# A Strassen matmul on one core: a pair of groups in another order, and small sums moved from GpSimd to VectorE

## The chip, the cores and the metric

The kernel runs on one core of a Trainium2 chip. The metric is the time of one execution on the device, in microseconds. Five engines work side by side, each with a queue of its own that it works through in order: TensorE (PE) multiplies, VectorE (DVE) and ScalarE (ACT) compute elementwise, GpSimd (POOL) does so more slowly, and SyncE (SP) issues the transfers. They wait for each other by semaphores that are set when the program is built.

## The reference

```
cs = np.cumsum(x, axis=1)                     # x: 8 x 2048 x 2048 float32
diff = cs - (cs shifted by one row, a zero row first)
return np.matmul(diff, w)                     # w: 2048 x 2048 float32
```

The difference of the running sum is x again, so the output is x times w, 16384 x 2048 by 2048 x 2048.

## The kernel before

**The arithmetic.** The rows of x are cut into 128 tiles of 128 rows. Four tiles are computed as plain products at the start while w is loaded, the next eight in two transitional groups; from then on 29 equal **groups** of four tiles follow (`Group`, L988). In a group the tiles are called g, h, k, l. Each tile's 2048 columns are cut in two halves, and w in four blocks, so that tiles g and k, or h and l, make a 2 x 2 block matrix. The group computes it by Strassen's scheme in Winograd's form: seven block products, P1 to P7, in place of eight. P1, P2, P3, P4 and P5 are cut once more in the same way, into seven quarters p1 to p7 each (a step of four matmuls of 128 x 512); P6 is computed whole, in eight steps of four matmuls; P7 is whole in even groups and by seven in odd ones (`onto`, L1082). Products accumulate in the eight PSUM banks (b0 to b7).

**A step's name.** `1:P1.p7` is quarter p7 of P1 in the odd group of a pair, `0:` the even group. What else stands around the matmuls:

- `load`, `weigh0/1`, `scale`, `recip`, `unit`, `narrow0/1`, `turn0/1`: a tile of x is loaded in two halves, ACT sums the absolute values of its rows (L125), DVE makes a scale of it (L141, L150) and POOL the factor for the way back (L155), ACT rounds the tile to f16 in place (L166), and a transposing transfer turns it (L179). SP issues loads, turns and the stores `put` (L612) from one queue.
- `S1` to `S4` are sums of whole tile halves, and `P1.s1` to `P5.s4`, `P7.s1` to `s4` the **small sums** of x of 128 x 512 in f16 that the inner seven need (`small_sums`, L1033). Each runs on DVE (L561) or, if its name stands in `ON_POOL`, on POOL (L559).
- `fp4` and the like: DVE makes a weight of 128 x 2048 for a quarter just in time, in the one buffer `flow` (L957).
- `cg`, `ct`, `cv` (L1056) and P7's `c1` to `c7` (L1088): ACT copies a partial product out of a bank, to another bank or to an SBUF buffer c. `m1`, `m2`, `a1` to `a7k` (L1063): DVE **merges** such a copy into a bank. A product's seven quarters go on in the same bank once copy or merge have read it.
- `keep` (ACT, L598 or L1118) starts an output piece in a buffer c from a bank, `add` (DVE, L601 or L1129) adds another bank to it, `last` (ACT, L598) scales it, `put` stores it. There are eight buffers c, taken and given back in the order in which the steps are written.

Where ACT and DVE read one bank after each other, the second waits for the first to end, as for a true dependence.

**What sets the order.** `Group` only makes a table of named steps. A list of names, `ORDER` (L1272), holds each step of a pair of groups once, with `+1` or `+2` for the pair whose step it is; the loop at L1367 goes through the list once per pair and runs each step's code, and so fills the queues of all five engines. `after` (L86) keeps each engine's instructions in the order of writing. 415 names make a pair. The last group's P4 has a list of its own, `END_ORDER`.

Of the kernel before, what the change touches and what calls it, by code (L numbers as in the profile page):

```python
# [10 lines left out]
def kernel(  # L11
# [1279 lines left out]
    1:scale.l+1 1:recip.l+1 1:narrow0.l+1 1:turn0.l+1 1:S1.g+1 1:keep.C11g1+1 1:P2.s4+1
    1:narrow1.l+1 0:last.C21g1+1 1:P2.p2+1 1:add.C11g0.v+1 1:put.C11g0+1 1:P2.p6+1
    1:P1.p4+1 1:turn1.l+1 0:add.C21h1.q+1 0:put.C21g1+1 1:P2.p5+1 1:S2.g+1
    1:add.C11g1.q+1 1:P6g.2+1 0:keep.C21h0+1 1:keep.C11h0+1 1:unit.l+1 1:P2.s3+1
    1:P2.p7+1 1:keep.C11h1+1 1:S4.g+1 1:P2.fp4+1 1:add.C11h1.q+1 1:P6g.3+1
    0:add.C21h0.x+1 1:add.C11h1.e+1 1:P5.p1+1 1:P6g.1+1 0:load.g+2 1:S1.h+1 1:P5.s1+1
    1:P5.cg+1 1:P2.p4+1 1:S2.h+1 0:last.C21h1+1 1:P2.p3+1 1:P5.p2+1 1:keep.C22g0+1
# [112 lines left out]
```

## Time and profile before

| | |
|---|---|
| three runs, median (lowest, highest) | 1508.2 us (1507.02, 1510.32) |
| profiled execution | 1507.86 us, of which the span 1505.6 us |
| PE busy | 1446.9 us, 96% |
| DVE, ACT, POOL busy | 1321.8, 1115.9, 460.9 us |
| granted clock of PE | 1.00 |
| transfers on SP's queue | 84.5% of 16 engines' span |

In the rows below, a group of instructions reads: line, engine, operation, output and inputs by the program's names, shapes, count, then busy time and mean duration in ns, then the idle time of the engine just before them and what ended it. A row of the table of waits has who waited, for whom, the total in us, how often, and the longest. A row of the timeline has start, duration, engine, line and operation, with the idle time ahead of it in brackets.

### The profile page before, as it was taken

To read this page: it belongs to the slowest core of one execution; us is meant where nothing else is said; L and a number is where in the kernel's file an instruction comes from. 1 tells how busy PE (TensorE), PEld (TensorE's weight loads), DVE (VectorE), ACT (ScalarE), POOL (GpSimd) and SP (SyncE) were. 2 spreads that over 40 slices of the span, in tenths; PEclk is the share of its full clock that TensorE was granted. 3 is DMA by queue.
4 is the path that set the end of the run, shared out by engine and by line. 5 is a ranking of instruction groups with operands and counts; after the bars stand their busy time and mean duration, and the time that the engine had idled before them with its cause. 6 is when DMAs were issued, how large, how long until landed. Compare 5 with 4: busy or idle time off the path is not lost. (4 is left out here: it accounts for less than half of the span.)

```text
span 1505.6 us, 20953 instructions
## 1 busy us (share of the span) xinstructions
PE 1446.9 (96%) x6617; PEld 644.1 (43%) x6623; DVE 1321.8 (88%) x2166; ACT 1115.9 (74%) x1726; POOL 460.9 (31%) x440
## 2 busy tenths in 40 slices
...
DMA packets 377760, 351.65 MB, mean 234 GB/s; under 512 B 274800, under 2 KB 274800, under 8 KB 377520
## 3 DMA queue, kind: packets, MB, share of 16 engines
q1 hardware_dynamic: 377088, 348.47, 84.5%
...
## 5 line engine op out<-in xcount | busy, mean ns | idle before, releaser
L590 PE MATMUL b<-W,x 128*128 128x512 f16 x2004 | 485.8, 379 | 14.6 <-DVE c L1129 8.9
L590 PEld LDWEIGHTS <-x 128*128 128x128 f16 x2712 | 263.5, 98 | 349.2 <-issue 26.7
L571 PE MATMUL b<-W,x 128*128 128x512 f16 x1696 | 393.5, 379 | 0.1
L1129 DVE TENSOR_TENSOR c<-b,c 128x512 f32<-128x512 f32 x504 | 337.5, 683 | 60.4 <-ACT c L1118 37.6
L166 ACT ACTIVATE F<-F,of 128x1024 f16<-128x1024 f32 x246 | 283.2, 1151 | 42.9 <-DVE of L150 40.2
L125 ACT ACTIVATE waste<-F 128x1024 uint8<-128x1024 f32 x246 | 259.5, 1055 | 37.1 <-DMA F<-in_x_dram 35.6
L590 PEld LDWEIGHTS <-inner 128*128 128x128 f16 x1816 | 176.8, 98 | 254.0 <-issue 25.6
L590 PE MATMUL b<-W,inner 128*128 128x512 f16 x1000 | 251.6, 379 | 26.9 <-DVE b L1063 22.3
L598 ACT ACTIVATE c<-b,of 128x512 f32<-128x512 f32 x268 | 178.3, 684 | 133.4 <-PE b L590 59.4
L571 PEld LDWEIGHTS <-x 128*128 128x128 f16 x1696 | 165.7, 98 | 200.9 <-DVE x L561 1.9
L601 DVE SCALAR_TENSOR_TENSOR c<-b,of,c 128x512 f32<-128x512 f32 x286 | 208.4, 744 | 24.9 <-ACT c L598 11.0
L561 DVE TENSOR_TENSOR x<-x,x 128x1024 f16<-128x1024 f16 (+1 forms) x345 | 208.4, 612 | 20.4 <-PE b L571 14.7
L559 POOL TENSOR_TENSOR inner<-x,inner 128x512 f16<-128x512 f16 x87 | 115.4, 1327 | 335.9 <-DVE inner L561 230.9
L590 PE MATMUL b<-flow,x 128*128 128x512 f16 x700 | 179.7, 379 | 3.8 <-DVE flow L957 3.3
L598 ACT ACTIVATE c<-c,of 128x512 f32<-128x512 f32 x224 | 158.6, 721 | 18.9 <-DVE c L1129 18.9
L1118 ACT COPY c<-b 128x512 f32<-128x512 f32 x224 | 127.6, 583 | 39.7 <-PE b L571 20.3
L559 POOL TENSOR_TENSOR inner<-x 128x512 f16<-128x512 f16 x58 | 76.6, 1320 | 261.0 <-DVE x L561 145.3
L1063 DVE TENSOR_TENSOR b<-b,c 128x512 f32<-128x512 f32 x200 | 137.1, 693 | 17.0 <-ACT c L1056 14.3
L155 POOL TENSOR_SCALAR of<-of,uw 128x1 f32<-128x1 f32 x124 | 74.5, 611 | 185.8 <-DVE of L141 178.3
L590 PE MATMUL b<-inner 128*128 128x512 f16 x472 | 118.7, 379 | 1.2 <-ACT c L598 0.8
L957 DVE TENSOR_TENSOR flow<-W 128x2048 f16<-128x2048 f16 x86 | 113.1, 1315 | 0.0
L559 POOL TENSOR_TENSOR inner<-inner,x 128x512 f16<-128x512 f16 x58 | 77.8, 1341 | 75.8 <-PE b L590 58.8
...
## 6 DMA issues: line engine op xcount, KB each, us to landing
...
out_dram<-c SPq DMA_DIRECT2D x492, 256.0 KB, 3.5
...
W<-in_x_dram SPq DMA_DIRECT2D x16, 256.0 KB, 7.1
...
out_dram<-o POOLq DMA_DIRECT2D x5, 256.0 KB, 4.0
out_dram<-o SPq DMA_DIRECT2D x5, 256.0 KB, 3.4
...
```

Of the source, the lines that this page charges most:

```text
L125: lambda: nc.scalar.activation(waste, where[t][i], ABS, scale=1.0 / ROW, accum_out=sums_of[t][:, i : i + 1],),
L166: lambda: nc.scalar.activation(narrowed(t)[:, ds(i * NH, NH)], where[t][i], COPY, scale=s),
L559: after("pool", lambda: nc.gpsimd.tensor_tensor(dst.all, p.all, q.all, op))
L561: after("dve", lambda: nc.vector.tensor_tensor(dst.all, p.all, q.all, op))
L571: said = nc.tensor.matmul(to[n], a[k], b[k][:, n, :], start=(first and k == 0), stop=(k == KH - 1), skip_group_check=True,)
L590: said = nc.tensor.matmul(to, a[k], b[k], start=(first and k == 0), stop=(k == 3), skip_group_check=True)
L598: after("act", lambda: nc.scalar.activation(c, p, COPY, scale=u))
L601: after("dve", lambda: nc.vector.scalar_tensor_tensor(c, p, u, c, MUL, ADD))
L957: after("dve", lambda: nc.vector.tensor_tensor(flow_all, x, y, op))
L1063: after("dve", lambda: nc.vector.tensor_tensor(t, p, s, ADD))
L1118: after("act", lambda: nc.scalar.copy(to, p))
L1129: after("dve", lambda: nc.vector.tensor_tensor(to, p, to, ADD))
```

## The change

Two tables are replaced, and no code. `ORDER` holds the same 415 names in another order (with `+0`, `+1` and `+2`, since the list begins at another point of the pair). `ON_POOL` holds 8 names in place of 21: six of the old ones and two new ones (1:P3.s3, 1:P7.s4), while fifteen become instructions of DVE. The lines after `ON_POOL` have numbers lower by two, those after `ORDER` by one: L561 is L559, L1063 is L1061, L1129 is L1127.

```diff
     ON_POOL = """
-    0:P1.s1 0:P1.s3 0:P1.s4 0:P2.s1 0:P2.s2 0:P2.s3 0:P2.s4 0:P3.s2 0:P4.s3 0:P5.s4
-    1:P2.s1 1:P2.s2 1:P2.s3 1:P2.s4 1:P3.s1 1:P3.s2 1:P3.s4 1:P4.s2 1:P4.s3 1:P4.s4
-    1:P5.s4
+    0:P1.s1 0:P2.s1 1:P3.s1 1:P3.s3 1:P3.s4 1:P4.s2 1:P4.s4 1:P7.s4
     """.split()
...
     ORDER = """
...
-    0:keep.C21h1+1 0:add.C12g1.e+1 0:keep.C21g0+1 0:add.C12h1.e+1 1:P1.s2+1 1:P1.p5+1
-    1:P1.cg+1 0:last.C12g1+1 1:unit.k+1 1:P1.s4+1 0:put.C22g0+1 0:P4.p6+1 0:put.C12h0+1
-    0:P4.s3+1 1:P1.ct+1 0:keep.C21g1+1 0:add.C21h1.e+1 1:P1.fp4+1 0:put.C22h1+1
-    1:P1.p6+1 1:load.l+1 1:turn0.k+1 1:narrow1.k+1 1:P1.s3+1 1:turn1.k+1 1:P1.m1+1
-    1:weigh0.l+1 0:add.C21g0.x+1 0:P4.p3+1 1:P1.p2+1 0:add.C21g1.x+1 1:P1.p7+1 1:P2.p1+1
...
-    0:recip.g+2 1:P7.fp6+1 1:P7.c5+1 1:keep.C12h1+1 1:P5.s4+1 1:P5.p6+1 1:P7.p2+1
-    1:P5.m1+1 1:add.C22g0.x+1 1:P7.s4+1 1:P7.p6+1 1:P5.p7+1 0:narrow0.g+2 0:narrow1.g+2
-    1:P7.a5g+1 1:P7.c6+1 1:P5.m2+1 1:P5.p3+1 1:put.C22g0+1 1:keep.C22h1+1 1:P4.p2+1
-    1:P3.s2+1 1:P3.s4+1 0:weigh1.h+2 1:add.C12h1.z+1 1:P7.a6+1 1:keep.C12h0+1
-    1:keep.C22g1+1 1:P3.p1+1 0:turn0.g+2 1:P7.fp4+1 1:add.C12g0.q+1 0:scale.h+2
-    0:turn1.g+2 1:last.C12g0+1 1:put.C12g0+1 1:P7.p3+1 1:add.C22g1.x+1 1:P7.p4+1
-    1:P7.fp7+1 1:P3.p3+1 1:add.C12g1.z+1 1:P3.p6+1 1:P7.p7+1 1:P4.p1+1 0:recip.h+2
...
+    0:add.C12g1.e+1 1:P1.s3+1 0:put.C22g0+1 0:P4.p1+1 0:P4.p3+1 0:put.C12h0+1
+    0:keep.C21g1+1 1:unit.h+1 0:keep.C21h1+1 0:add.C12h1.e+1 0:add.C21h1.e+1
+    0:last.C12g1+1 1:P2.s1+1 1:P1.s2+1 1:P1.cg+1 1:P1.p5+1 1:P1.s4+1 0:keep.C21g0+1
+    1:narrow1.k+1 1:P1.ct+1 1:P1.p6+1 0:add.C21g1.x+1 1:load.l+1 0:P4.p6+1 1:P1.p2+1
+    1:P1.m1+1 0:add.C21g0.x+1 0:last.C12h1+1 1:P2.s2+1 0:add.C21g1.q+1 1:turn1.k+1
+    1:P1.fp4+1 1:turn0.k+1 1:P2.p1+1 1:P1.p7+1 1:P1.m2+1 1:P2.s3+1 1:P2.cv+1
...
+    1:P7.p5+1 0:weigh1.h+2 1:P7.c1+1 1:P7.a1+1 1:last.C11g1+1 1:P5.p5+1 1:P7.fp6+1
+    1:P5.s4+1 1:keep.C12g1+1 0:scale.h+2 1:put.C11h1+1 1:P5.ct+1 1:P7.c5+1 1:P5.p6+1
+    1:unit.l+1 1:P5.m1+1 0:recip.g+2 1:P7.p2+1 1:add.C22g0.x+1 1:P3.s1+1 1:P7.a5g+1
+    0:put.C21h0+1 1:P7.s4+1 1:P7.p6+1 1:put.C11g1+1 1:P5.p7+1 1:P4.p2+1 1:P7.c6+1
+    1:P5.p3+1 1:keep.C12h1+1 0:recip.h+2 1:P7.a6+1 1:P3.s3+1 1:P5.m2+1 1:put.C22g0+1
+    0:narrow0.g+2 0:unit.g+2 1:keep.C12h0+1 1:keep.C22h1+1 1:P7.fp4+1 1:keep.C22g1+1
+    1:P3.s2+1 1:P7.p3+1 0:turn0.g+2 1:add.C12h1.z+1 1:add.C22g1.x+1 1:P7.p4+1
+    1:put.C22g1+1 1:P3.p1+1 1:P3.s4+1 1:P7.fp7+1 0:narrow1.g+2 1:add.C12g0.q+1
+    0:narrow0.h+2 1:P3.p3+1 1:add.C12g1.z+1 0:narrow1.h+2 1:last.C12g0+1 1:P7.p7+1
...
```

**DVE around the odd group's merge P1.m1.** The first row is add.C12h1.e of the even group; b2 is the bank of add.C21h1.e, `flow<-W,S` is P1.fp4, the L1063 row is P1.m1. Before:

```order
L1129 TENSOR_TENSOR c2_755<-b7_791,c2_755 128x512
L561 TENSOR_TENSOR inner_779<-inner_779,x00_63 128x512
L561 TENSOR_TENSOR inner_779<-x00_63,inner_779 128x512
L1129 TENSOR_TENSOR c5_767<-b2_786,c5_767 128x512
L957 TENSOR_TENSOR flow_783<-W_58,S1_775 128x2048
L561 TENSOR_TENSOR inner_779<-x00_63,x10_65 128x512
L1063 TENSOR_TENSOR b2_786<-b5_789,c3_759 128x512
```

And of the change, with P1.s3 (`x00_63,x10_65`) as the first row and P1.fp4 as the last:

```order
L559 TENSOR_TENSOR inner_779<-x00_63,x10_65 128x512
L1127 TENSOR_TENSOR c1_751<-b3_787,c1_751 128x512
L1127 TENSOR_TENSOR c0_747<-b2_786,c0_747 128x512
L559 TENSOR_TENSOR inner_779<-x11_66 128x512
L559 TENSOR_TENSOR inner_779<-inner_779,x00_63 128x512
L559 TENSOR_TENSOR inner_779<-x00_63,inner_779 128x512
L1127 TENSOR_TENSOR c3_759<-b7_791,c3_759 128x512
L1061 TENSOR_TENSOR b2_786<-b4_788,c5_767 128x512
L599 SCALAR_TENSOR_TENSOR c2_755<-b0_784,of_8085,c2_755 128x512
L559 TENSOR_TENSOR inner_779<-inner_779,x01_64 128x512
L1127 TENSOR_TENSOR c3_759<-b6_790,c3_759 128x512
L955 TENSOR_TENSOR flow_783<-W_58,S1_775 128x2048
```

P1.fp4 and P1.s3 stood between add.C21h1.e and the merge; now P1.s3 is ahead of the add and P1.fp4 behind the merge.

**ACT at the same place.** The copy that reads the bank b2 is keep.C21g1; the first L1056 row is P1.cg, the second P1.ct. Before:

```order
L1118 COPY c5_767<-b1_785 128x512
L598 ACTIVATE c4_763<-b6_790,of_8073 128x512
L1056 COPY b7_791<-b5_789 128x512
L598 ACTIVATE c1_751<-c1_751,of_7858 128x512
L1056 COPY c3_759<-b1_785 128x512
L1118 COPY c0_747<-b2_786 128x512
```

And of the change, where the L1054 rows are the same two copies (keep.C21g1 is the first row):

```order
L1116 COPY c3_759<-b2_786 128x512
L1116 COPY c0_747<-b5_789 128x512
L596 ACTIVATE c4_763<-c4_763,of_7854 128x512
L1054 COPY b5_789<-b4_788 128x512
L596 ACTIVATE c2_755<-b6_790,of_8085 128x512
L166 ACTIVATE F_62<-F_62,of_8386 128x1024
L1054 COPY c5_767<-b3_787 128x512
```

keep.C21g1 was the last of the six and is now the first of the seven; narrow1.k (L166) now stands ahead of P1.ct.

**DVE from the odd group's merges P7.a5g to P7.fp7.** Before (the rows are P7.a5g, P5.m2, add.C12h1.z, P7.a6, P7.fp4, add.C12g0.q, scale.h, add.C22g1.x, P7.fp7):

```order
L1063 TENSOR_TENSOR b2_786<-b2_786,c5_767 128x512
L1063 TENSOR_TENSOR b0_784<-b6_790,c3_759 128x512
L1129 TENSOR_TENSOR c1_751<-b0_784,c1_751 128x512
L1063 TENSOR_TENSOR b2_786<-b2_786,c4_763 128x512
L957 TENSOR_TENSOR flow_783<-W_58,flow_783 128x2048
L1129 TENSOR_TENSOR c0_747<-b0_784,c0_747 128x512
L141 TENSOR_SCALAR of_8623<-of_8623 128x1
L601 SCALAR_TENSOR_TENSOR c4_763<-b2_786,of_8390,c4_763 128x512
L957 TENSOR_TENSOR flow_783<-W_58 128x2048
```

And of the change (P7.a5g, recip.h, P7.a6, P5.m2, P7.fp4, P3.s2, add.C12h1.z, add.C22g1.x, P7.fp7):

```order
L1061 TENSOR_TENSOR b2_786<-b2_786,c6_771 128x512
L150 RECIPROCAL of_8617<-of_8617 128x1
L1061 TENSOR_TENSOR b2_786<-b2_786,c2_755 128x512
L1061 TENSOR_TENSOR b1_785<-b0_784,c4_763 128x512
L955 TENSOR_TENSOR flow_783<-W_58,flow_783 128x2048
L559 TENSOR_TENSOR inner_779<-inner_779,x01_64 128x512
L1127 TENSOR_TENSOR c1_751<-b1_785,c1_751 128x512
L599 SCALAR_TENSOR_TENSOR c0_747<-b2_786,of_8386,c0_747 128x512
L955 TENSOR_TENSOR flow_783<-W_58 128x2048
```

add.C12h1.z moves from ahead of P7.a6 and P7.fp4 to behind them, and the small sum P3.s2, which POOL did, stands between.

**POOL from the odd group's P3.s1 on.** Of the change (P3.s1, P7.s4, P3.s3, unit.g, P3.s4, P4.s2, P4.s4, then P1.s1 and P2.s1 of the next even group):

```order
L557 TENSOR_TENSOR inner_779<-x11_66 128x512
L557 TENSOR_TENSOR inner_779<-x00_63,inner_779 128x512
L557 TENSOR_TENSOR x11_66<-x01_64,x11_66 128x512
L155 TENSOR_SCALAR of_8588<-of_8588,uw_59 128x1
L557 TENSOR_TENSOR inner_779<-x01_64,inner_779 128x512
L557 TENSOR_TENSOR x20_67<-x20_67,x21_68 128x512
L557 TENSOR_TENSOR x30_69<-x21_68,x20_67 128x512
L557 TENSOR_TENSOR inner_779<-x10_65 128x512
L557 TENSOR_TENSOR inner_779<-x11_66 128x512
```

These eight are all the sums that POOL does in a pair, where it did 21; the others are now L559 rows of DVE, as in the places above.

More of the change, by code (lines that the diff above doesn't have):

```diff
@@ L1291 @@
[L1291 to L1297, printed above, removed]
@@ new lines @@
+    1:turn0.g+1 0:P5.s3+1 0:add.C12g0.z+1 0:P3.s2+1 0:P3.s4+1 1:weigh1.h+1 1:turn1.g+1
+    0:P5.m1+1 0:last.C12g0+1 0:last.C11g1+1 1:weigh0.h+1 0:P5.fp4+1 1:scale.h+1
+    1:recip.h+1 0:P6h.3+1 0:P3.p6+1 0:add.C12g1.q+1 0:put.C11g1+1 0:P6h.2+1 0:P5.p7+1
+    0:P5.p3+1 0:P3.p7+1 0:keep.C12h0+1 0:add.C22g0.x+1 0:P5.m2+1 0:put.C12g0+1
+    0:keep.C12h1+1 0:P4.s1+1 0:S3.h+1 0:keep.C22h1+1 0:put.C11h0+1 0:add.C12h1.z+1
+    0:add.C12h1.q+1 0:keep.C22g1+1 0:P5.p4+1 1:narrow0.h+1 0:P4.fp4+1 0:P7h.2+1
```

89 lines of the change are left out of this document (44 added, 45 removed).

## The prediction

> **What bounds the kernel now.** First the page, for who is busy; then the groups of instructions with shapes kept apart, for where TensorE (PE) stands idle; then the table of waits; then the chain of waits, for the length of one pair of groups; last the timeline of the two places where PE stands longest.
>
> ```profile
> span 1505.6 us, 20953 instructions
> ...
> PE 1446.9 (96%) x6617; PEld 644.1 (43%) x6623; DVE 1321.8 (88%) x2166; ACT 1115.9 (74%) x1726; POOL 460.9 (31%) x440
> ```
>
> The profiled execution took 1507.86 us, 2.3 us more than its span; I make the sum against it. The median of the three runs is 1508.2 us, 0.3 us higher. PE sets the end, but VectorE (DVE) is at 88%.
>
> ```profile
> 1192.80 3.45 PE b L571 x16
> ...
> 1228.87 7.07 PE b L590 x32
> ...
> 1320.36 7.07 PE b L590 x32
> ...
> 1412.72 7.07 PE b L590 x32
> ```
>
> The first row gives PE's pace: 3.45 us for 16 matmuls, 0.216 us each, so 0.863 us for a step of four. A pair of groups has 51 + 50 steps (each of P1 to P5 has seven per group, P6 eight, P7 eight in the even and seven in the odd group), 101 x 0.863 = 87.1 us. The other three rows are the same stretch of three successive pairs: (1412.72 - 1228.87) / 2 = 91.9 us. So nearly 5 us of each pair is PE standing still.
>
> ```profile
> L590 PE MATMUL b<-W,x 128*128 128x512 f16 x2004 | 485.8, 379 | 14.6 <-DVE c L1129 8.9 <-DVE b L1063 4.5 <-ACT c L598 0.8
> ...
> L590 PE MATMUL b<-W,inner 128*128 128x512 f16 x1000 | 251.6, 379 | 26.9 <-DVE b L1063 22.3 <-ACT c L1118 3.3 <-DVE c L1129 0.2
> ...
> L590 PE MATMUL b<-flow,x 128*128 128x512 f16 x700 | 179.7, 379 | 3.8 <-DVE flow L957 3.3
> ```
>
> ```profile
> DVE c L1129 <- ACT c L1118: 37.6, 29, 2.3
> ...
> PE b L590 <- DVE b L1063: 26.8, 20, 1.9
> ...
> PE b L590 <- DVE c L1129: 9.2, 16, 0.7
> ...
> PE b L590 <- ACT c L1118: 3.3, 13, 0.3
> PE b L590 <- DVE flow L957: 3.3, 14, 0.2
> ```
>
> The three groups have 45.3 us of idle PE. A matmul's row is 0.379 us long where the pace is 0.216, so each wait hides another 0.163 us; 20 + 16 + 13 + 14 waits hide 10.3 us. Together about 55 us: the most that any order can win. Four fifths of it is DVE being late: the merges (L1063) and the adds (L1129).
>
> One pair, at the odd group's P1.p7 (DVE, ACT, GpSimd and PE in turn):
>
> ```profile
> 1040.01 0.42 DVE L561 TENSOR_TENSOR inner<-x,inner 128x512 f16<-128x512 f16 x1
> 1042.47 0.69 DVE L1129 TENSOR_TENSOR c<-b,c 128x512 f32<-128x512 f32 x1 [2.04 <-ACT c L1118]
> 1043.08 1.22 DVE L957 TENSOR_TENSOR flow<-W,S 128x2048 f16<-128x2048 f16 x1
> 1044.21 1.38 DVE L561 TENSOR_TENSOR inner<-x,x 128x512 f16<-128x512 f16 x1
> 1045.51 0.69 DVE L1063 TENSOR_TENSOR b<-b,c 128x512 f32<-128x512 f32 x1
> ...
> 1041.84 0.60 ACT L1118 COPY c<-b 128x512 f32<-128x512 f32 x1
> ...
> 1043.12 2.19 POOL L559 TENSOR_TENSOR inner<-inner,x 128x512 f16<-128x512 f16 x1 [3.43 <-PE b L590]
> ...
> 1041.96 1.03 PE L590 MATMUL b<-S,inner 128*128 128x512 f16 x4
> 1042.83 1.89 PE L590 MATMUL b<-W,x 128*128 128x512 f16 x8
> 1046.25 1.02 PE L590 MATMUL b<-W,inner 128*128 128x512 f16 x4 [1.54 <-DVE b L1063]
> ```
>
> Read it backwards. P1.p7 waits 1.54 us (1.70 with the hidden part) for merge P1.m1. The merge is late because three instructions stand ahead of it on DVE: P1.fp4, the small sum P1.s3, and add.C21h1.e, for which DVE stood idle 2.04 us until ACT's copy keep.C21g1 had read the same bank. P1.s3 took 1.38 us, about a microsecond too long, while a sum of GpSimd (POOL), itself 2.19 us long, stood beside it.
>
> **The change part by part.**
>
> (a) The wait at P1.p7. Between P1.p6 and P1.p7 PE now has P4.p6, P1.p2 and P2.p1, 3 x 0.863 = 2.59 us instead of 1.73. On ACT keep.C21g1 is ahead of P1.cg and P1.ct rather than behind them, and on DVE three small sums and an add stand between add.C21h1.e and the merge, while P1.fp4 and P1.s3 are out of the way. After P1.p6 the merge has at most one add, 0.68, and itself, 0.69, to go: 1.4 us, well under 2.59. I take the whole 1.70 us as gone, in 14 odd groups: -23.8 us. Bounds: half of it stays (-11.9), if the merge is then late for P1.ct instead; the other end is the value itself.
>
> (b) The waits at P3.p1 and P7.p4 of the odd group.
>
> ```profile
> 1073.00 0.69 DVE L1129 TENSOR_TENSOR c<-b,c 128x512 f32<-128x512 f32 x1 [0.81 <-ACT c L598]
> ...
> 1073.75 1.02 PE L590 MATMUL b<-W,x 128*128 128x512 f16 x4 [0.57 <-DVE c L1129]
> ...
> 1075.86 1.04 PE L590 MATMUL b<-flow,x 128*128 128x512 f16 x4 [0.23 <-DVE flow L957]
> ```
>
> Here merge P5.m2, ACT's keep.C22h1 and DVE's add.C12h1.z use one bank in turn, 0.69 us each, behind P5.p7, and P3.p1 needs that bank: 2.1 us and the hops against two steps, 1.73. Now four steps stand between P5.p7 and P3.p1 (3.45 us), and P7.fp4 and P3.s2 run on DVE while ACT reads: 0.69 + 1.22 + 0.42 + 0.69 = 3.0. The wait of 0.57 + 0.16 goes: 14 x 0.73 = -10.2 us. P7.p4 has four steps since P7.p6 where it had five, but its weights (P7.fp4) no longer stand behind add.C12h1.z: copy 0.6, P7.a6 0.69, P5.m2 0.69, P7.fp4 1.22 make 3.2 us against 3.45. Its 0.23 + 0.16 goes too: 14 x 0.39 = -5.5 us. Bounds for both together: 0 and -15.7; they go where the DVE queue has no new delay, so I take the full value and put the delay into (c).
>
> (c) A new loop through a result buffer. P7.fp7 now stands behind add.C22g1.x, this behind keep.C22g1 on ACT, and that one needs the buffer that put.C22g0 frees: in the old order keep.C22g1 took a buffer that DVE had freed.
>
> ```profile
> out_dram<-c SPq DMA_DIRECT2D x492, 256.0 KB, 3.5
> ```
>
> From P5.p5 to P7.p7: two ACT copies 1.1, P5.m1 0.69, add.C22g0.x 0.74, the landing 3.5, keep 0.69, add 0.74, P7.fp7 1.22, the hops some 0.4: 9.1 us. PE has ten steps between, 8.63 us. So 0.5 us of new stall, and the DVE work queued behind (P5.fp4, the P7 merges, the adds that free the next group's banks) is late with it; I take 0.8 us a pair, 14 x 0.8 = +11.2 us. Bounds: 0, if the landing is a microsecond shorter than the median; and 0.8 + 2.1 us a pair, +41 us, if it takes the 5.6 us that the page gives for a load of twice the bytes.
>
> (d) POOL does 8 small sums of a pair where it did 21 (two of the eight are new to it), so DVE does 13 more.
>
> ```profile
> L559 POOL TENSOR_TENSOR inner<-x,inner 128x512 f16<-128x512 f16 x87 | 115.4, 1327 | 335.9 <-DVE inner L561 230.9 <-PE b L590 103.7
> ...
> L957 DVE TENSOR_TENSOR flow<-W 128x2048 f16<-128x2048 f16 x86 | 113.1, 1315 | 0.0
> ...
> L957 DVE TENSOR_TENSOR flow<-W,inner 128x2048 f16<-128x2048 f16 x58 | 70.8, 1220 | 15.5 <-PE b L590 15.5
> ...
> L559 POOL TENSOR_TENSOR inner<-x,x 128x512 f16<-128x512 f16 x44 | 50.9, 1157 | 0.0
> ...
> L561 DVE TENSOR_TENSOR inner<-x 128x512 f16<-128x512 f16 x73 | 41.9, 574 | 3.4 <-DMA x<-F 2.4
> ...
> L561 DVE TENSOR_TENSOR inner<-x,x 128x512 f16<-128x512 f16 x16 | 16.3, 1017 | 0.0
> L561 DVE TENSOR_TENSOR x<-x 128x512 f16<-128x512 f16 x30 | 12.5, 418 | 0.0
> ```
>
> POOL's sums (five groups, 304 in all; the first and the last are shown) become 8 x 14 plus two for the last even group, 114: 190 fewer. An undisturbed sum is 418 ns on DVE: 190 x 0.418 = +79 us. Against that, DVE's f16 instructions run long where POOL works: 86 x (1315 - 1220) + 73 x (574 - 418) + 16 x (1017 - 418) ns = 29 us; in proportion 190/304 of it, 18 us, goes. Net +61 us of DVE time, 4.3 us a pair. One stretch of a pair's length shows what room there is (PE, its weight loads, DVE, ACT, POOL):
>
> ```profile
> 1032.00:1123.50 91.50, 88.72 (x407) 39.61 (x406) 80.86 (x135) 70.00 (x111) 30.89 (x29) 1.00 0.83 226
> ```
>
> DVE is idle 10.6 us of it, so the 4.3 lie in waits that it has anyway: on the path I count 0. If that cover is gone it costs up to 61 us.
>
> The Trainium skill, "SBUF — State Buffer", section "Who interferes with whom", says that a VectorE instruction with two SBUF inputs and a GpSimd instruction that reads SBUF exclude each other, the first to issue holding the shared port to its end. The 1.38 and the 2.19 us above agree with it. It also speaks against this change: it makes a rival below.
>
> (e) The head, before the pairs, and the last P4 keep their code: 0. SP's puts and turns keep their number; what a put's new place costs is in (c).
>
> Sum: 1507.9 - 23.8 - 10.2 - 5.5 + 11.2 = 1479.6. I say **1480 us**.
>
> **Rivals.**
>
> *The locks gather.* Of the eight sums left, P3.s4, P4.s2, P4.s4 of the odd and P1.s1, P2.s1 of the next even group stand close together, in the stretch of loop (c), beside P7.fp7, P5.fp4 and DVE's own sums. If one full POOL sum, 1.16 us at worst and about 1.0 as P1.s3 showed, falls on the path in each pair: +14 us, 1494. For it: P3.s4 follows P3.s2 directly. Against: adds from PSUM stand between, and the 8 leave fewer chances than the 21. The rule of the Trainium skill named above ("SBUF — State Buffer", "Who interferes with whom") would bring it about.
>
> *PE at its floor.* Landings are short, (c) is nothing, and the small waits go too: 1507.9 - 55 = 1453. For it: all waits named were lateness of DVE. Against: (c) is short by arithmetic.
>
> *The landing decides.* keep.C22g1 waits for slow landings, (c) at some 2.8 us a pair: 1479.6 + 28 = 1508, no change. For it: DMA stands in the way of a merge for the first time. Against: the median is 3.5.
>
> *DVE paces.* The moved sums stand right ahead of merges and adds that PE waits for, so each is paid: 0.418 x 14 = 5.9 us for each of the 13. From the fifth on it eats the gain of 28; with nine of them on the path, 1479.6 + 53 = 1532, slower. For it: DVE goes from 88% to about 93% of a shorter span. Against: in the places shown the sums stand before the merge's own PE step ends.
>
> **How the numbers follow.** Forecast (1470 to 1490) 0.45; locks 0.17; floor 0.16; landing 0.09; DVE 0.13. A change of under 0.2%, 3 us, can't be told from none. The first three are faster, and of the landing case a little: faster 0.79, same 0.07, slower 0.14. The range: the floor case half in, from 1460; the locks and most of the landing case in, to 1505; left out are the lower half of the floor case and the DVE case.
>
> **What would show it.** (a): no wait for L1061 (the merges' new line) of over a microsecond ahead of the odd P1.p7, and no 2 us of idle DVE at add.C21h1.e. (b): no PE wait at the odd P3.p1. (c): ACT idle at keep.C22g1 on "DMA out_dram", then a short PE wait at P7.p7 or the next even P2. (d): DVE near 1380 us busy, POOL near 190. A pair near 90 us. I am wrong if a pair is still 91.5 or more, if DVE's idle per pair stays near 11 us, or if PE's new wait at P7.p7 is over 2 us.

## The result and the profile after

| | before | changed |
|---|---|---|
| median (lowest, highest) | 1509.26 us (1507.02, 1510.68), 4 runs | 1487.55 us (1487.19, 1489.84), 4 runs |
| profiled execution | 1507.86 us | 1489.84 us |

The changed kernel takes 0.986 of the time before, interval 0.984 to 0.988: 21.7 us less, where 28 were predicted (1480 us). Its profiled execution is the slowest of its four runs, 18.0 us below the one of before.

From the page of the changed kernel:

```profile
span 1488.1 us, 20871 instructions
...
PE 1445.2 (97%) x6617; PEld 641.6 (43%) x6623; DVE 1354.4 (91%) x2356; ACT 1129.8 (76%) x1726; POOL 220.9 (15%) x250
...
q1 hardware_dynamic: 377088, 348.47, 88.1%
...
L588 PE MATMUL b<-W,x 128*128 128x512 f16 x2004 | 479.2, 379 | 15.4 <-DVE x L559 4.9 <-DVE of L150 3.8 <-ACT b L1054 3.2
...
L588 PE MATMUL b<-W,inner 128*128 128x512 f16 x1000 | 252.0, 380 | 0.8 <-DVE b L1061 0.5 <-DVE c L1127 0.2
...
L588 PE MATMUL b<-flow,x 128*128 128x512 f16 x700 | 179.8, 379 | 4.3 <-DVE flow L955 3.2
```

The same three groups of matmuls as in the prediction have 20.5 us of idle PE where they had 45.3. Nearly all of the gain is in `W,inner`, the group of P1.p7: 26.9 us have become 0.8. `flow,x`, the group of P7.p4, has not moved (3.8 before), and `W,x` has as much as before, but behind other work: no longer behind adds, but behind sums of x, merges (L150 is recip.g, which follows the merge P5.m1 on DVE) and copies of ACT.

The table of waits of the changed kernel:

```profile
ACT c L1116 <- DMA out_dram<-c: 45.8, 43, 2.3
...
ACT c L596 <- DMA out_dram<-c: 40.2, 49, 2.4
...
DVE x L559 <- DMA x<-F: 13.6, 16, 2.1
...
DVE c L1127 <- ACT c L1116: 6.9, 14, 0.8
...
PE b L588 <- DVE flow L955: 5.1, 17, 0.7
PE b L588 <- DVE x L559: 4.9, 5, 1.7
```

DVE waits 6.9 us for ACT's copies where it waited 37.6: the queueing for a bank is gone. In its place ACT waits 86 us for result buffers, that is for stores to land; in the kernel before these waits were 11.3 us in all (8.6, 2.2 and 0.5). Most of them cost PE nothing, as an experiment below shows.

Where the time of a pair went can be seen if the 101 steps of a pair are laid over the rows of the matmuls and the idle time ahead of each step is taken (with the 0.16 us that a wait hides, as in the prediction), a mean over 13 pairs (a few matmul records are missing, so a small wait may be put one step off). The third column belongs to an experiment below, the changed kernel with half of every store left out:

| idle PE ahead of, us a pair | before | changed | changed, half stores |
|---|---|---|---|
| odd P1.p7 | 1.76 | 0.00 | 0.00 |
| odd P3.p1 | 0.75 | 0.06 | 0.06 |
| odd P7.p4 | 0.38 | 0.40 | 0.40 |
| odd P7.p7 | 0.00 | 0.07 | 0.07 |
| odd P5.p7 | 0.00 | 0.53 | 0.49 |
| odd P7.p5 and p6, even P5.p1 | 0.10 | 0.77 | 0.01 |
| all other steps | 1.57 | 1.43 | 0.10 |
| sum | 4.56 | 3.26 | 1.13 |

The place of step (a) in one pair of the changed kernel, DVE's timeline. The second row holds add.C12h1.e and add.C21h1.e, the L1061 row is the merge P1.m1:

```profile
1120.11 0.41 DVE L559 TENSOR_TENSOR inner<-x,x 128x512 f16<-128x512 f16 x1
1120.44 1.36 DVE L1127 TENSOR_TENSOR c<-b,c 128x512 f32<-128x512 f32 x2
1121.72 0.41 DVE L559 TENSOR_TENSOR inner<-x 128x512 f16<-128x512 f16 x1
1122.06 0.42 DVE L559 TENSOR_TENSOR inner<-inner,x 128x512 f16<-128x512 f16 x1
1122.86 0.43 DVE L559 TENSOR_TENSOR inner<-x,inner 128x512 f16<-128x512 f16 x1 [0.38 <-PE b L588]
1123.20 0.69 DVE L1127 TENSOR_TENSOR c<-b,c 128x512 f32<-128x512 f32 x1
1124.35 0.70 DVE L1061 TENSOR_TENSOR b<-b,c 128x512 f32<-128x512 f32 x1 [0.47 <-ACT c L1054]
```

No 2.04 us of idle DVE ahead of the add, the first row (P1.s3) takes 0.41 us where it took 1.38, and the merge waits only for ACT's own copy.

The place of step (b) in the group whose stores are shown next, on PE (P7.p4, then P3.p1, which no longer waits):

```profile
1061.85 1.04 PE L588 MATMUL b<-flow,x 128*128 128x512 f16 x4 [0.23 <-DVE flow L955]
1062.78 1.02 PE L588 MATMUL b<-W,x 128*128 128x512 f16 x4
```

And the stores and turns, in the view of transfers, for three short stretches of one pair, the one of the fourteen in which P5.p1 waits longest. A row has what is moved, the queue, the count, KB each and the median time from issue to landing. The stretch 1058 to 1060 us, when keep.C22g1's buffer is stored (put.C22g0):

```profile
out_dram<-c SPq DMA_DIRECT2D x1, 256.0 KB, 2.3
```

1073 to 1077 us, four stores of the odd group and the load of a tile l:

```profile
out_dram<-c SPq DMA_DIRECT2D x4, 256.0 KB, 5.7
F<-in_x_dram SPq DMA_DIRECT2D x2, 512.0 KB, 7.7
```

1078.5 to 1081.5 us, the even group's turns of tile k, issued right behind them:

```profile
x<-F SPq DMA_TRANSPOSE x2, 6.5
```

The store that is issued alone lands after 2.3 us (2.3 or 2.4 in all fourteen pairs). Here four in a burst land after 5.7 and the turns behind them after 6.5, where the page has a median of 3.4; over the fourteen pairs the burst's stores have a median of 5.1, turn0.k of 5.5 and turn1.k of 3.9. What this does, on DVE (the first of the sums S1.g, S2.g) and, from the timeline of PE, on P5.p1:

```profile
1086.82 1.42 DVE L559 TENSOR_TENSOR x<-x,x 128x1024 f16<-128x1024 f16 x2 [2.14 <-DMA x<-F]
```

```profile
1087.57 1.04 PE L588 MATMUL b<-W,x 128*128 128x512 f16 x4 [1.71 <-DVE x L559]
```

The Trainium skill, "DMA: Bandwidth & Descriptors", section "Queues, rings and completion order", says that each of the 16 transfer engines takes the descriptors of a ring in their order. The burst agrees with it: here the four stores, the load and the two turns land in the order in which SP issued them, the last turn last.

But these turns were as slow in the kernel before, where five stores and the load stand ahead of them. The same two turns there, and P5.p1 of the same group, which didn't wait:

```profile
x<-F SPq DMA_TRANSPOSE x2, 5.9
```

```profile
1100.24 1.03 PE L590 MATMUL b<-W,x 128*128 128x512 f16 x4
```

Over all pairs turn0.k and turn1.k land after 4.9 and 4.4 us there (medians), in the changed kernel after 5.5 and 3.9. What the new order has changed is the time that is left: from the issue of turn1.k to P5.p1 it was 6.6 us and is 4.7 (medians), of which the sum S1.g takes 0.7. In the changed kernel P5.p1 waits over 0.1 us in the six groups whose turn1.k takes more than 4 us, and in no other.

### The profile page after: what moved, and what is told of

It reads as the page before. It is cut to its first block, busy times and chain, and to the rows that moved or that the text cites. A ratio compares the mean times of both kernels' runs of the same rounds, so it can differ in the third digit from the quotient of the medians.

```text
span 1488.1 us, 20871 instructions
## 1 busy us (share of the span) xinstructions
PE 1445.2 (97%) x6617; PEld 641.6 (43%) x6623; DVE 1354.4 (91%) x2356; ACT 1129.8 (76%) x1726; POOL 220.9 (15%) x250
## 4 chain that ended last, share of the span: by engine, by line
PE 39%; DMA 19%; DVE 19%; ACT 13%; issue 7%; SPq 2%; ACTq 0%; DVEq 0%
PE b L588 23%; PE b L569 14%; DMA out_dram<-c 8%; DMA F<-in_x_dram 6%; DVE c L599 4%; DMA x<-F 4%; ACT F L166 4%; ACT waste L125 4%; DVE c L1127 3%; DVE x L559 3%; ACT c L596 3%; DVE b L1061 3%; DVE flow L955 3%; PE b L283 2%; DVE inner L559 2%
## 5 line engine op out<-in xcount | busy, mean ns | idle before, releaser
L1127 DVE TENSOR_TENSOR c<-b,c 128x512 f32<-128x512 f32 x504 | 339.2, 683 | 28.8 <-PE b L588 14.9
L166 ACT ACTIVATE F<-F,of 128x1024 f16<-128x1024 f32 x246 | 280.5, 1146 | 29.1 <-DVE of L150 26.4
L559 DVE TENSOR_TENSOR x<-x,x 128x1024 f16<-128x1024 f16 (+1 forms) x360 | 212.2, 596 | 17.2 <-DMA x<-F 13.6
L155 POOL TENSOR_SCALAR of<-of,uw 128x1 f32<-128x1 f32 x124 | 58.2, 481 | 767.1 <-DVE of L141 759.2
L1061 DVE TENSOR_TENSOR b<-b,c 128x512 f32<-128x512 f32 x200 | 135.7, 691 | 13.7 <-ACT c L1054 10.2
L557 POOL TENSOR_TENSOR inner<-x 128x512 f16<-128x512 f16 x44 | 65.2, 1483 | 309.5 <-PE b L588 227.8
L955 DVE TENSOR_TENSOR flow<-W 128x2048 f16<-128x2048 f16 x86 | 104.5, 1215 | 0.1
L559 DVE TENSOR_TENSOR inner<-x,inner 128x512 f16<-128x512 f16 x103 | 54.7, 531 | 18.3 <-PE b L588 17.6
L955 DVE TENSOR_TENSOR flow<-W,inner 128x2048 f16<-128x2048 f16 x58 | 70.5, 1216 | 0.0
```

Of the source, the lines that this page charges most:

```text
L166: lambda: nc.scalar.activation(narrowed(t)[:, ds(i * NH, NH)], where[t][i], COPY, scale=s),
L557: after("pool", lambda: nc.gpsimd.tensor_tensor(dst.all, p.all, q.all, op))
L559: after("dve", lambda: nc.vector.tensor_tensor(dst.all, p.all, q.all, op))
L955: after("dve", lambda: nc.vector.tensor_tensor(flow_all, x, y, op))
L1061: after("dve", lambda: nc.vector.tensor_tensor(t, p, s, ADD))
L1127: after("dve", lambda: nc.vector.tensor_tensor(to, p, to, ADD))
```

## The experiments

All were timed beside the kernel before; ratios are to it, with their intervals, and a difference given in us is a difference of ratios times 1508 us. In the cuts of `ORDER` below lines of the list are joined, so that only the names that move are seen. Waits in us a pair are taken as in the table above.

| run | ratio to before | interval |
|---|---|---|
| changed kernel | 0.9861 | 0.9844 to 0.9878 |
| old_order_new_sums | 1.0110 | 1.0096 to 1.0124 |
| new_order_old_sums | 0.9914 | 0.9901 to 0.9926 |
| old_order_merge_first | 0.9958 | 0.9945 to 0.9972 |
| old_order_sum_first | 0.9929 | 0.9911 to 0.9947 |
| two_sums_back | 0.9862 | 0.9847 to 0.9877 |
| half_puts | 0.9705 | 0.9685 to 0.9725 |
| half_puts_before | 0.9943 | 0.9925 to 0.9960 |
| half_burst | 0.9785 | 0.9770 to 0.9799 |
| tail_order | 0.9885 | 0.9863 to 0.9906 |
| tail_two | 0.9954 | 0.9939 to 0.9969 |
| tail_three | 0.9976 | 0.9964 to 0.9987 |
| tail_two_half_puts | 0.9732 | 0.9719 to 0.9746 |

**The two halves of the change.** The kernel before with the new list of sums:

```diff
     ON_POOL = """
-    0:P1.s1 0:P1.s3 0:P1.s4 0:P2.s1 0:P2.s2 0:P2.s3 0:P2.s4 0:P3.s2 0:P4.s3 0:P5.s4
-    1:P2.s1 1:P2.s2 1:P2.s3 1:P2.s4 1:P3.s1 1:P3.s2 1:P3.s4 1:P4.s2 1:P4.s3 1:P4.s4
-    1:P5.s4
+    0:P1.s1 0:P2.s1 1:P3.s1 1:P3.s3 1:P3.s4 1:P4.s2 1:P4.s4 1:P7.s4
```

> The old ORDER with the new, shorter list of GpSimd sums, so the one half of the change alone. Theory A (the order takes the waits away, the list only shortens the locks): the small sum P1.s3 no longer lasts 1.38 us, so the merge P1.m1 comes some 0.9 us sooner and the odd P1.p7 waits 0.8 us in place of 1.70; the waits at P3.p1 and P7.p4 stay. 14 x 0.9 = 13 us less: about 1496 us, DVE busy 1355. Theory B (the shorter list is the gain, the order does next to nothing): all of it, 1488 us. Theory C (DVE paces): thirteen more sums a pair stand ahead of its merges in an order that was not made for them: 1515 us or more.

Measured 1524.4 us, 1.1% slower than before (16.6 us): theory C. Its table of waits:

```profile
PE b L588 <- DVE b L1061: 20.2, 21, 1.9
...
PE b L588 <- DVE c L1127: 17.8, 47, 1.8
```

The wait at the odd P1.p7 does shrink, from 1.76 to 1.13 us a pair, though not to the 0.8 of theory A. But PE now waits 47 times for adds where it waited 16 times, and the idle PE of a pair rises from 4.56 to 5.99 us. In the old order thirteen more sums stand ahead of adds and merges that PE needs.

The other half, the changed kernel with the old list (the same lines with + and - exchanged):

> The new ORDER with the old list of 21 GpSimd sums, the other half alone. Theory A: no 2 us of idle DVE and no wait at the odd P1.p7 and P3.p1, but the locks are back, some 2 us of longer DVE instructions a pair where it has 0.8 now, of which half reaches PE: 1488 + 14 x 1.0 = about 1502 us. Theory B: no gain, 1508 us. Theory C: better than the change itself, since DVE has 80 us less to do: 1480 us.

Measured 1495.3 us, 13 us faster than before and 7 us better than theory A, to which it is nearest: the order gives three fifths of the gain alone, and the list, which costs 16.6 us in the old order, gives 8 in the new one. Its table of waits and DVE's timeline in the odd group (P7.fp6, P3.s3, P5.m2, P7.fp4):

```profile
PE b L590 <- DVE flow L957: 22.4, 14, 1.7
```

```profile
1057.19 1.81 DVE L957 TENSOR_TENSOR flow<-W,flow 128x2048 f16<-128x2048 f16 x1
...
1061.96 1.03 DVE L561 TENSOR_TENSOR x<-x,x 128x512 f16<-128x512 f16 x1
1062.91 0.69 DVE L1063 TENSOR_TENSOR b<-b,c 128x512 f32<-128x512 f32 x1
1063.52 1.57 DVE L957 TENSOR_TENSOR flow<-W,flow 128x2048 f16<-128x2048 f16 x1
```

Nearly all that it loses is at the odd P7.p4, 1.76 us a pair (1.6 of them visible): three instructions ahead of it take 1.81 (1.63 in most pairs), 1.03 and 1.57 us, where they take 1.22, 0.42 and 1.22 with POOL at rest. In return the odd P5.p7 no longer waits, since POOL does its P5.s4 here.

**Step (a) alone, in the old order.** First only the merge is moved ahead of the weight and the sum:

```diff
-    0:keep.C21g1+1 0:add.C21h1.e+1 1:P1.fp4+1 0:put.C22h1+1 1:P1.p6+1 1:load.l+1
-    1:turn0.k+1 1:narrow1.k+1 1:P1.s3+1 1:turn1.k+1 1:P1.m1+1
+    0:keep.C21g1+1 0:add.C21h1.e+1 0:put.C22h1+1 1:P1.p6+1 1:load.l+1
+    1:turn0.k+1 1:narrow1.k+1 1:turn1.k+1 1:P1.m1+1 1:P1.fp4+1 1:P1.s3+1
```

> The kernel before, with two names moved: 1:P1.fp4 and 1:P1.s3 stand right behind the merge 1:P1.m1, nothing else is changed. Step (a) of the prediction alone. If the odd P1.p7's wait is worth what its row says, 1.70 us in 14 pairs: 1509 - 24 = 1485 us. Rival: the weight and the sum are now late themselves or the merge waits for ACT's copies behind the same bank, and half is given back: 1497 us.

Measured 1502.6 us, 6 us less, half of what even the rival gives. P1.p7 reads the small sum P1.s3 itself, and now it waits for that. The table of waits:

```profile
PE b L590 <- DVE inner L561: 17.1, 16, 2.1
```

Then the sum stands ahead of the add, in DVE's idle time, and only the weight behind the merge:

```diff
-    0:keep.C21g1+1 0:add.C21h1.e+1 1:P1.fp4+1 0:put.C22h1+1 1:P1.p6+1 1:load.l+1
-    1:turn0.k+1 1:narrow1.k+1 1:P1.s3+1 1:turn1.k+1 1:P1.m1+1
+    0:keep.C21g1+1 1:P1.s3+1 0:add.C21h1.e+1 0:put.C22h1+1 1:P1.p6+1 1:load.l+1
+    1:turn0.k+1 1:narrow1.k+1 1:turn1.k+1 1:P1.m1+1 1:P1.fp4+1
```

> The kernel before, with 1:P1.s3 moved ahead of 0:add.C21h1.e, into the time in which DVE waits for ACT's copy, and 1:P1.fp4 behind the merge 1:P1.m1. In the run with the merge first, the odd P1.p7 still waited 1.20 us, now for the small sum P1.s3, which it reads itself. This run takes both away, so it is step (a) of the prediction alone. If (a) is worth its row: the wait at P1.p7 of 1.76 us a pair goes and nothing else moves, 1509 - 14 x 1.76 = 1484 us. Rival (given back): the time that PE wins is waited for at the next places where DVE is late, the odd P3.p1 and P7.p4 and the even P5.p7: 1495 us or more.

Measured 1496.3 us: 11 us less, and not 24, as the rival has it, though at another place than it names. The wait at P1.p7 is gone, but the next step, P2.p1, which needs the bank that add.C21g0.x frees, now waits 0.70 us a pair:

```profile
PE b L590 <- DVE c L601: 7.7, 15, 0.8
```

and the even P5.p7 another 0.1. So the mechanism of (a) holds, and in the old order about half of its price is given back, most of it one step later. The new order has moved add.C21g0.x as well, ahead of P1.fp4, and there P2.p1 doesn't wait.

**Two sums taken from GpSimd.** In the changed kernel P5.p7 waits for the merge P5.m1. One pair of it, DVE (P7.fp6, P5.s4, scale.h, P5.m1), POOL (P3.s1) and PE (P5.p7 with P4.p2):

```profile
874.16 1.22 DVE L955 TENSOR_TENSOR flow<-W,flow 128x2048 f16<-128x2048 f16 x1
875.29 1.37 DVE L559 TENSOR_TENSOR inner<-x,inner 128x512 f16<-128x512 f16 x1
876.59 0.20 DVE L141 TENSOR_SCALAR of<-of 128x1 f32<-128x1 f32 x1
876.71 0.68 DVE L1061 TENSOR_TENSOR b<-b,c 128x512 f32<-128x512 f32 x1
...
874.62 1.76 POOL L557 TENSOR_TENSOR inner<-x 128x512 f16<-128x512 f16 x1 [17.35 <-PE b L588]
...
877.45 1.89 PE L588 MATMUL b<-W,x 128*128 128x512 f16 x8 [0.32 <-DVE of L150]
```

P5.s4 takes 1.37 us in place of 0.42, since POOL's P3.s1 comes in behind the weight, and the merge is 0.95 us late. So it is in eleven of the fourteen pairs; in the other three the weight P7.fp6 takes 1.66 to 2.12 us in its place. The run gives P3.s1, and P7.s4 after it, to DVE:

```diff
-    0:P1.s1 0:P2.s1 1:P3.s1 1:P3.s3 1:P3.s4 1:P4.s2 1:P4.s4 1:P7.s4
+    0:P1.s1 0:P2.s1 1:P3.s3 1:P3.s4 1:P4.s2 1:P4.s4
```

> The changed kernel with two GpSimd sums given to DVE, 1:P3.s1 and 1:P7.s4, which stand beside DVE's P7.fp6 and P5.s4. Theory L (the lock): P7.fp6 takes 1.22 us in place of 1.65 and P5.s4 0.42, the merge P5.m1 is in time, and the waits at the odd P7.p6 and P5.p7 (0.18 and 0.53 us a pair) go: 1488 - 10 = about 1478 us. Rival Q (the length of the queue): DVE's two sums, 0.33 us each, delay P7.a5g, P7.a6 and P7.fp4 by as much as the locks did, so the wait only moves to P7.p4: 1486 to 1490 us.

Measured 1487.5 us: no change, as rival Q has it. P5.p7 no longer waits; P7.p4 waits 0.86 us a pair where it waited 0.40, and P7.p3 ahead of it 0.43 where it waited for nothing. The table of waits, and DVE's row of P7.s4:

```profile
PE b L588 <- DVE flow L955: 9.8, 14, 0.7
```

```profile
876.14 1.06 DVE L559 TENSOR_TENSOR inner<-x,inner 128x512 f16<-128x512 f16 x1
```

The two sums cost 0.33 us each, and P7.s4 another 0.64, because POOL now does P3.s3 beside it. From P7.fp6 to P7.fp4 DVE is hardly idle, so whatever is put in there comes out at P7.p3 and P7.p4. What the stretch would do with no lock in it at all was left to the runs on the tail below.

**Stores of half the width.** In the changed kernel and, as a control, in the kernel before:

```diff
-        after("sp", lambda: nc.sync.dma_start(out2[ds(t * P, P), ds(at * NB, NB)], c))
+        after("sp", lambda: nc.sync.dma_start(out2[ds(t * P, P), ds(at * NB, NB // 2)], c[:, ds(0, NB // 2)]))
```

> The changed kernel with stores of half the width (128 x 256 of each 128 x 512 result piece; the other half of the output is left out). Theory D (transfers in line): in the changed kernel four stores and a load are issued in the 3.5 us ahead of the even group's turns turn0.k and turn1.k, which then land 5.8 to 7.2 us after their issue where the median is 3.3, and S1.g, P5.p1 and the scattered waits behind late results follow. With half the bytes to store these go, 0.8 us or more a pair: 1488 - 11 = 1477 us or below. Theory E (DVE alone is what is left): within 3 us of 1488.

> The same half-width stores in the kernel before, as a control. In its order hardly any ACT instruction waits for a store (2.2 + 8.6 us in all) and S1.g has its turns in time: within 3 us of 1509. If stores cost the kernel before as much as theory D says of the changed one, 1498.

Measured 1462.5 us, 23.5 us less than the changed kernel, and 1498.6 us, 8.6 less than before. Theory D holds, and more strongly than expected: the new order pays almost three times as much for its stores as the old one. The control missed its own forecast: the old order pays for its stores too, 8.6 us and not under 3. PE's waits in the changed kernel with half stores:

```profile
PE b L588 <- DVE of L150: 3.4, 11, 0.7
PE b L588 <- DVE flow L955: 3.3, 14, 0.2
PE b L588 <- DVE b L1061: 1.1, 3, 0.5
```

Only the odd tail is left, P5.p7 and P7.p4 (third column of the table above); nearly every scattered wait of the changed kernel is gone, the even P5.p1 with them. The length of a pair, from the same wait at P7.p4 in the timeline of PE, here eleven pairs apart; first with half stores, then in the changed kernel:

```profile
246.46 1.04 PE L588 MATMUL b<-flow,x 128*128 128x512 f16 x4 [0.23 <-DVE flow L955]
...
1218.83 1.04 PE L588 MATMUL b<-flow,x 128*128 128x512 f16 x4 [0.23 <-DVE flow L955]
```

```profile
248.35 1.04 PE L588 MATMUL b<-flow,x 128*128 128x512 f16 x4 [0.23 <-DVE flow L955]
...
1245.21 1.04 PE L588 MATMUL b<-flow,x 128*128 128x512 f16 x4 [0.23 <-DVE flow L955]
```

972.37 / 11 = 88.4 us against 996.86 / 11 = 90.6. Without half of the stores' bytes the change is worth 0.9705 / 0.9943 = 0.976, 36 us; with them 21 us. That half takes back 15 us.

Only the four stores ahead of the even group's turns at half width:

```diff
-            self.step(f"put.{c}", lambda: put(self.at.pop(c), self.row(c), n))
+            burst = self.more and c in ("C22h0", "C12g1", "C21g0", "C22h1")
+            store = half_put if burst else put
+            self.step(f"put.{c}", lambda: store(self.at.pop(c), self.row(c), n))
```

> The changed kernel with half-width stores for four of the 32 result pieces of a pair only (odd C22h0, C12g1, C21g0, C22h1, the four that are issued just ahead of the even group's turns; half of these pieces of the output is left out). Theory B (the burst): the turns land 1.8 us sooner, S1.g and P5.p1 wait no more and the pair is 0.7 us or more shorter: 1488 - 10 = 1478 us or below. Rival S (spread): the other waits for stores and turns stay, and an eighth of what all half-width stores gave is won: 1488 - 3 = 1485 us.

Measured 1476.5 us, 11.5 us less than the changed kernel: theory B. An eighth of the stores gives half of what all of them give, and the even P5.p1 waits no more: turn0.k and turn1.k land after 3.4 and 3.1 us (medians, 5.5 and 3.9 in the changed kernel). That is 0.47 of the 0.96 us a pair that PE waits less; the rest is spread over small waits of the even group. ACT still waits 80 us for result buffers (86 in the changed kernel), so buffers that come free sooner can be only the smaller part of the gain. It is not the amount of traffic alone, then, but its place: these bytes stand ahead of turns that PE needs soon after their issue. Whether an order that issues turn1.k earlier, as the old one does, would win as much with whole stores was not tried.

**The odd group's tail.** Can the waits at P5.p7 and P7.p4 be ordered away? First:

```diff
-    0:P1.s1 0:P2.s1 1:P3.s1 1:P3.s3 1:P3.s4 1:P4.s2 1:P4.s4 1:P7.s4
+    0:P1.s1 0:P2.s1 1:P3.s3 1:P3.s4 1:P4.s2 1:P4.s4 1:P7.s4
...
-    1:P7.c1+1 1:P7.a1+1 1:last.C11g1+1 1:P5.p5+1 1:P7.fp6+1 1:P5.s4+1 1:keep.C12g1+1
+    1:P7.c1+1 1:P5.s4+1 1:P7.a1+1 1:last.C11g1+1 1:P5.p5+1 1:P7.fp6+1 1:keep.C12g1+1
...
-    1:add.C22g0.x+1 1:P3.s1+1 1:P7.a5g+1 0:put.C21h0+1 1:P7.s4+1
+    1:add.C22g0.x+1 1:P7.a5g+1 0:put.C21h0+1 0:unit.g+2 1:P7.s4+1
...
-    0:narrow0.g+2 0:unit.g+2 1:keep.C12h0+1 1:keep.C22h1+1 1:P7.fp4+1 1:keep.C22g1+1
+    0:narrow0.g+2 1:keep.C12h0+1 1:keep.C22h1+1 1:P7.fp4+1 1:P3.s1+1 1:keep.C22g1+1
```

> The changed kernel with three names moved and one sum less on GpSimd: 1:P5.s4 stands ahead of 1:P7.a1, where DVE waits 0.9 us for ACT's copy; 1:P3.s1 is done by DVE behind 1:P7.fp4; 0:unit.g stands ahead of 1:P7.s4, so that GpSimd does P7.s4 only after DVE's P7.fp6. Theory: the merges and weights of the odd group's P5 and P7 are then 0.7 us earlier, and the waits there (P5.p7 0.53, P7.p4 0.40, P7.p6 0.18, P7.p5 0.13 us a pair) go: 1488 - 14 x 1.1 = 1472 us. Rival: one of the moved sums is late or waits for a buffer itself, or P7.p7 takes over: 1482 us or more.

Measured 1490.4 us; by the ratios 3.6 us slower than the changed kernel, with intervals that overlap. (In this run P3.s1 adds a tile that P3.s3 has already overwritten, so that its values are not those of the reference; the work is the same.) DVE's P7.fp6, and POOL beside it:

```profile
1054.88 2.16 DVE L955 TENSOR_TENSOR flow<-W,flow 128x2048 f16<-128x2048 f16 x1
```

```profile
1054.80 1.16 POOL L557 TENSOR_TENSOR inner<-x,inner 128x512 f16<-128x512 f16 x1 [2.44 <-PE b L588]
1055.91 2.14 POOL L557 TENSOR_TENSOR x<-x,x 128x512 f16<-128x512 f16 x1
```

The weight takes 2.16 us: with P3.s1 gone POOL did P7.s4 and P3.s3 there. unit.g had not held them back, since it needs only scale.g, which is long done. P7.p6 waits 0.82 us for it, and P3.p1 now waits 0.52. The Trainium skill, "SBUF — State Buffer", section "Who interferes with whom", gives the rule, an exclusive hold on a shared port; these rows agree: POOL's sum starts 0.08 us ahead of the weight, and the weight is 0.94 us longer than its 1.22.

Second, with unit.h, which needs the later scale.h, ahead of POOL's sums, and P3.s3 behind P3.s4:

```diff
-    1:P7.c1+1 1:P7.a1+1 1:last.C11g1+1 1:P5.p5+1 1:P7.fp6+1 1:P5.s4+1 1:keep.C12g1+1
+    1:P7.c1+1 1:P5.s4+1 1:P7.a1+1 1:last.C11g1+1 1:P5.p5+1 1:P7.fp6+1 1:keep.C12g1+1
...
-    1:add.C22g0.x+1 1:P3.s1+1 1:P7.a5g+1 0:put.C21h0+1 1:P7.s4+1
+    1:add.C22g0.x+1 1:P7.a5g+1 0:put.C21h0+1 0:unit.h+2 1:P7.s4+1 1:P3.s1+1
...
-    1:P7.a6+1 1:P3.s3+1 1:P5.m2+1
+    1:P7.a6+1 1:P5.m2+1
...
-    1:P3.s4+1 1:P7.fp7+1
+    1:P3.s4+1 1:P3.s3+1 1:P7.fp7+1
...
-    0:unit.h+1 0:P1.p7+1
+    0:P1.p7+1
```

> The changed kernel with four names moved and the same eight GpSimd sums: 1:P5.s4 stands ahead of 1:P7.a1, where DVE waits 0.9 us for ACT's copy; on GpSimd 0:unit.h, which needs DVE's scale.h, comes ahead of 1:P7.s4, so that its sums start only when DVE's P7.fp6 is done; 1:P3.s1 follows 1:P7.s4, and 1:P3.s3 follows 1:P3.s4. In the run with the other order of this tail P7.fp6 took 2.16 us, because GpSimd did P7.s4 and P3.s3 beside it (unit.g had not held them back); here nothing is beside it. Theory: P7.fp6 takes 1.22 us, P5.m1 is in time, the waits of the odd P5.p7 and P7.p4 (0.9 us a pair) go: 1488 - 13 = 1475 us. Rival (transfers decide): with PE 0.9 us faster a pair the same transfers come later against it, and half or more is given back: 1481 us or more.

Measured 1501.8 us, 14 us slower than the changed kernel: more than all of the gain was lost, where the rival has half or more. The tail did what was wanted: P7.fp6 takes 1.21 us, P5.p7 doesn't wait, P7.p4 0.17 us. But the even P1.p2 and P2.p2 now wait 1.33 and 0.52 us a pair. In the table of waits (first PE's, then that of SP's queue):

```profile
PE b L588 <- ACT b L1054: 20.9, 19, 2.2
```

```profile
SPq L179 <- POOL x L557: 38.1, 14, 2.7
```

The changed kernel has no row like the second: 14 times, 2.7 us each, a turn waits for a GpSimd sum. P3.s3 reads x01, the tile that the next group's turn1.g fills; moved behind P3.s4, and lengthened by P7.fp7 beside it, it ends late. The turn is late, and with it the load that needs the turn's buffer, ACT's weigh0.k and the copy P1.cg behind it, and PE's P1.p2. Each of these waits is in the trace; that undoing the one move of P3.s3 would bring the tail's gain back was not tried.

Third, tail_two with two of ACT's copies moved ahead of what waits for transfers (the lines are those of tail_two):

```diff
-    0:weigh0.k+2 0:P1.cg+2 0:P1.p2+2
+    0:P1.cg+2 0:weigh0.k+2 0:P1.p2+2
...
-    1:keep.C21g1+1 0:recip.k+2 1:add.C21g1.q+1 1:add.C21h1.e+1 0:P2.cv+2 0:P2.p2+2
+    0:P2.cv+2 1:keep.C21g1+1 0:recip.k+2 1:add.C21g1.q+1 1:add.C21h1.e+1 0:P2.p2+2
```

> The run with the shorter tail (tail_two), with two more of ACT's names moved: 0:P1.cg stands ahead of 0:weigh0.k, which waits for load.k, and 0:P2.cv ahead of 1:keep.C21g1, which waits for a result buffer, that is for the landing of put.C22h0. In tail_two the tail's own waits went, but PE waited 1.33 us a pair at the even P1.p2 for P1.cg and 0.52 at P2.p2 for P2.cv. Theory D (what the tail won was lost to copies that stand behind transfers on ACT's queue): these two waits go, 1502 - 14 x 1.85 = 1476 us, below the changed kernel. Rival (the transfers are late for whoever is next): P1.ct and S1.g take their place, 1488 us or more.

Measured 1503.3 us: the rival's time, but its mechanism only in part. P1.p2's wait is gone, and P2.p1 waits 1.36 us a pair, for an add that stands behind ACT's keep.C21g1. Followed back, keep.C21g1 waits for the landing of put.C22h0 in eight of thirteen pairs. In the other five no transfer is in the chain: keep.C21g1 is late because P1.cg, weigh0.k, weigh1.k and P2.cv now stand ahead of it on ACT, and the trace still shows 0.8 us of wait at P2.p1. So more than half of this wait is the price of the move itself.

Last, tail_two with half stores:

> The shorter tail (tail_two) with all stores at half the width, as in the run half_puts (the other half of the output is left out). With full stores the same tail made the kernel 14 us slower. Theory D (the tail's gain was real, and the transfers took it back): without the stores in line it shows, half_puts less its waits at the odd P5.p7 and P7.p4: 1462.5 - 14 x 0.8 = about 1451 us, a pair of 87.6 us. Rival (the tail's new order costs by itself, by other names than transfers): 1470 us or more, as much slower than half_puts as tail_two was than the changed kernel.

Measured 1465.9 us, between the two: 4 us above half_puts, where tail_two was 14 above the changed kernel. Most of the loss went with the stores, the rest did not: the late turn1.g and its load are there with half stores too, and P1.p2 still waits 0.75 us a pair, about as much as the tail has won (0.7). No run here beats the changed kernel with its whole output.

## Why the prediction was right, and where it was not

**What bounds.** Right: PE's waits for DVE decided, and the gain came out of them. The signs named for it came too: DVE's idle time of a pair fell from 10.9 to 7.5 us, and a pair takes 90.6. The bound of 55 us was never approached with whole stores; with half stores 44 us were reached.

**(a)** Right in its full value: 1.76 us to 0.00, 14 x 1.76 = 24.6 us against 23.8. That it holds in full depends on the rest of the order: alone in the old order it was worth 11.

**(b)** Half right. P3.p1 went from 0.75 to 0.06, 9.7 us against 10.2. P7.p4 did not move (0.38, 0.40), and 5.5 us were counted for it. The step took P7.fp4 to be free once add.C12h1.z was out of its way, and began its chain at ACT's copy. But DVE is late there from further up: P7.fp6 or P5.s4 ahead of it, lengthened by POOL, P5.m1 behind them, and hardly any idle time to catch up in. In two_sums_back what was put into that stretch came out at P7.p3 and P7.p4.

**(c)** Wrong in its place, and too small. The loop that it names did not close: ACT is idle ahead of keep.C22g1 in no pair, and P7.p7 waits 0.07 us, with half stores too. put.C22g0 lands in 2.3 us there, and the working took the page's median of 3.5; its own lower bound, a landing a microsecond shorter, was the true case. Elsewhere transfers cost more than the 0.8 us a pair, in two ways. The largest wait, the even P5.p1, is for a turn behind stores, which no term had. Small waits of the even group (P2.p2, P2.p6, P3.p2, P3.p4), followed back, end at a store's landing for which ACT waited: the kind of wait that (c) names, at other places. In the profiled executions it is 3.26 - 1.13 = 2.1 us a pair between the changed kernel and half stores, and 4.56 - 3.93 = 0.6 between the same two of the old order: the new order brought 1.5 us a pair, 21 us, where the term was 11.2. By the medians of all runs it is the 15 us above, since the profiled execution of the changed kernel is the slowest of its runs and that of half_puts the fastest.

**(d)** Right that it costs nothing on the path in the new order; wrong as a general price, as the old order with the new list shows (+16.6 us). DVE's busy time rose by 32.6 us and not by 61; POOL's is 220.9 us and not near 190. A sum was priced by its row, 0.418 us; but sums that follow each other start 0.33 to 0.34 us apart (1121.72 and 1122.06 above), so 190 of them make 63 us. And locks gave back more than 18: the four groups of weights lost 16 us, 262.2 to 246.2, and the excess of the small sums over 0.418 us fell from 22.8 to 9.0.

**What was left out.** The small waits of the even group. The steps outside (a) and (b) had 1.57 us in the old order; with half stores 0.97 of it stay in the old order and 0.10 in the new one. So about 0.9 us a pair went that no term had counted, some 12 us. Followed back, most of these waits of the old order (even P1.p5, P2.p3 and P2.p5, odd P4.p4) end at an add or a weight that was late on DVE. The likeliest case had only the waits named; the case of PE at its floor had the others too.

**The sum.** By these terms a gain of 24.6 + 9.7 + 12 and a loss of 1 (P7.p7), 7 (P5.p7) and 21 (transfers) make 17 us, and the profiled executions, from which all these terms come, differ by 18.0; the medians differ by 21.7. That the predicted 28 was near is partly luck: 5.5 us of gain (P7.p4) did not come, 7 us (P5.p7) and some 10 (transfers) of loss were not counted, and neither were 12 us of gain (the small waits).

**The rivals.** The locks: P5.p7's 0.5 us a pair is one, at another place than named and half as dear. DVE as the pace: true of the old order, not of the new. The landing: the strongest of the four, and the one with the least chance; transfers decided over the rest of the gain, though not at keep.C22g1. PE at its floor: half_puts, 88.4 us a pair against 87.1, shows that the order itself comes near it.
